# Both output projections as seven block products over float32 quadrants in SBUF, and the next layer's first unit started at its second token half

## The chip, the cores and the metric

One core of a Trainium2 chip runs the whole program. The metric is the time that the device needs for one execution, in microseconds (us); a profile of one execution shows where it goes. TensorE (PE in the profile, with PEld for its weight loads) multiplies, VectorE (DVE), ScalarE (ACT) and GpSimd (POOL) do everything elementwise, and SyncE (SP) and ACT issue the DMAs.

## The reference

A decoder trunk of two layers on 1024 tokens of width 1024, in float32. Each layer normalises its input, multiplies it with a wide input matrix, runs several gated branches (attention, a short convolution in layer 0, cross-attention to 256 memory tokens) and multiplies their concatenated outputs, 1024 x 2048, with an output matrix:

```python
def odd_layer(h, mem, norm_g, w_in, w_out, ...):
    u = rms_norm(h, norm_g)
    proj = u @ w_in
    ...
    y = jnp.concatenate([yc * jax.nn.silu(cz), yx * jax.nn.silu(xz)], axis=-1)
    return h + y @ w_out
```

`even_layer` ends alike. `h + y @ w_out`, once in each layer, is the output projection.

## The kernel before

All matrix products are made at float32 precision out of float32r matmuls: each operand is split into a high part (ACT copies it to float32r, line 130) and a low part (the difference, line 131, on VectorE or GpSimd), and three products, high x high, high x low and low x high, are added up in PSUM. So each 128x128x512 piece of a product costs three matmuls.

The stages follow each other in program order: `run` goes through layer 0's eight heads of differential attention with the convolution groups between them, two pairs of cross-attention heads (`x_pair`), then `out_proj`; then layer 1's twelve heads, its two pairs and its `out_proj`. A scheduler orders the instructions of each engine by priority and readiness; each engine then runs its queue strictly in that order, and so do the DMA queues of SP and ACT. A tile that shares a buffer (same tag) with an older one waits until the older one's readers are done.

`u`, the normalised input, lies transposed in four tiles of 16 KB a partition (tag `u`: high and low parts, two token halves). A unit of an input projection reads it: `token_unit` for queries, keys and values (lines 200 to 202), `feature_unit` for gates and convolution (233 to 235), which goes over a token half at a time.

The attention writes its gated outputs `y` to DRAM (`y_dr`, in tiles of 256 tokens by 512 features). In layer 0 the first eight heads still have to be multiplied with a per-token norm (`on_dr`), which is loaded as a tile `rn` repeated over all partitions.

`out_proj` goes over the output's left half of columns two token blocks at a time, then over the right half a token block at a time. For each token block `out_blocks` loads four tiles of y (`yr`, on ACT's queue), multiplies them with `rn` where needed (GpSimd, line 753), splits them (ACT, VectorE) and issues 48 matmuls (lines 760 to 762). The left half's weights go into the four `u` tiles, and the first four of their sixteen chunks already into small free tiles during the last pair of cross-attention heads (`out_early`, called from `x_pair`). The right half's weights are loaded and split during the first half, into 32 tiles `wo`. The residual is loaded as `hb`, added to the PSUM bank (784, 802) and stored. After each token block of the right half in layer 0, `norm_rows` and `turn_rows` normalise the finished rows and transpose them into the next layer's `u`. The last block's transposes follow the third block of layer 1's first unit.

PSUM has eight banks under four tags: `d` 3, `s` 2, `t` 2, `o` 1. The attention uses `s` for scores, `t` for transposes and `o` for its output `po`, which VectorE gates (`y`, line 453) before the next `po` may start.

Of the kernel before, what the change touches and what calls it, by code (L numbers as in the profile page):

```python
# [7 lines left out]
F32 = mybir.dt.float32  # L8
# [25 lines left out]
class Trunk:  # L34
    def __init__(self, ctx, tc, io):
# [24 lines left out]
        self.queue, self.groups, self.boot, self.turn_last = [], 0, True, None  # L60
# [79 lines left out]

    def turn_rows(self, xn, dst_hi, dst_lo):

        nc = self.nc
        for j in range(2):
            tp = self.bank("pt", "t")
            for i in range(4):
                c = 4 * j + i
                nc.tensor.transpose(tp[:, i * P:(i + 1) * P], xn[:, c * P:(c + 1) * P], self.ident)
# [40 lines left out]
    def token_unit(self, weights, lhs_hi, lhs_lo, nblk, post, together=False):  # L189
# [5 lines left out]
        for t0 in range(0, nblk, step):  # L195
            blks = [(tb, self.bank("pd", "ds"[tb % 2] if together or self.boot else "d"), lhs_hi(tb), lhs_lo(tb)) for tb in range(t0, t0 + step)]
# [9 lines left out]
            if self.turn_last is not None and t0 == 2:  # L206
                with self.tc.issue_after(mm.ins):
                    self.turn_last()
                self.turn_last = None
# [246 lines left out]
    def qkv_unit(self, w, cols, ng, gs, g, extra=None, pairs=False, weights=None):  # L456
# [3 lines left out]
        qns = []  # L460

        def post(tb, ps):
            raw = self.evac(ps, 384 if extra is None else 396)
            qns.append(self.qk_norm(raw, ng, gs))
# [4 lines left out]
            if tb % 2:  # L469
                if pairs:  # L470
                    self.later(DEFER, lambda: self.qk_transpose_pairs(qns[tb - 1:tb + 1], (qh, ql), (kh, kd, kl, kz), g, (tb - 1) * P))
                else:
                    self.later(DEFER, lambda: self.qk_transpose(qns[tb - 1:tb + 1], [(qh, ql, g), (kh, kl, None)], (tb - 1) * P))
        if weights is None:
            weights = self.unit_weights(w, [(c, P) for c in cols] + ([] if extra is None else [extra[0]]), None if extra is None else (nc.vector, nc.gpsimd))
        self.token_unit(weights, self.u_lhs(0), self.u_lhs(1), NB, post)
# [112 lines left out]
    def x_pair(self, layer, pr, w, cq, cz, w_out):  # L589
# [23 lines left out]
        if pr == 1:  # L613
            self.out_early(w_out)
# [100 lines left out]
    def out_weights(self, w, half, tiles, chunks, raws):  # L715

        nc = self.nc
        for c in chunks:
            raw = raws()
            nc.sync.dma_start(out=raw, in_=w[c * P:(c + 1) * P, half * 512:(half + 1) * 512])  # L720
            self.split(tiles(0, c), tiles(1, c), raw, nc.vector if c % 2 else nc.gpsimd)

    def raw_tile(self):
        return self.pa.tile([P, 512], F32, name="wraw", tag="raw", bufs=4)

    def out_early(self, w):

        early = [[], []]
        for part, n in enumerate(("kd", "kz") if self.ptb == 2 else ("kd", "kd")):
            early[part].append(self.att_half(n))  # L730
            early[part].append(self.pk.tile([P, 512], F32R, name="we", tag="gate", bufs=2))
        for t in ("c1", "bias"):
            two = self.pk.tile([P, T + 4] if t == "c1" else [P, T], F32R, name="we", tag=t, bufs=1)
            for part in range(2):
                early[part].append(two[:, part * 512:(part + 1) * 512])
        self.early = early
        self.out_weights(w, 0, lambda part, c: early[part][c], range(len(early[0])), self.raw_tile)

    def out_blocks(self, layer, tbs, tiles, fetch=None):

        nc = self.nc
        pss = [self.bank("pd", "s" if i % 2 and tb > 1 else "d") for i, tb in enumerate(tbs)]
        for j in range(4):
            if fetch is not None:
                fetch(range(4 * j, 4 * j + 4))
            for tb, ps in zip(tbs, pss):
                ts = slice(tb * P, (tb + 1) * P)
                yr = self.pk.tile([P, 4, P], F32, name="yr2", tag="yr", bufs=4)
                nc.scalar.dma_start(out=yr, in_=self.y_dr[layer][tb // 2][j][tb % 2])
                if layer == 0 and j < 2:  # L750
                    rn = self.pa.tile([P, 4, P], F32, name="rn", tag="hs", bufs=3)
                    nc.scalar.dma_start(out=rn, in_=self.on_dr[j][tb].unsqueeze(0).broadcast_to([P, 4, P]))
                    nc.gpsimd.tensor_tensor(out=yr, in0=yr, in1=rn, op=ALU.mult)
                yh = self.pa.tile([P, 4, P], F32R, name="yh2", tag="wfh", bufs=3)
                yl = self.pa.tile([P, 4, P], F32R, name="yl2", tag="wfl", bufs=3)
                self.split(yh, yl, yr, nc.vector)
                for i in range(4):
                    c = 4 * j + i
                    h, l = tiles(0, c), tiles(1, c)
                    nc.tensor.matmul(ps, lhsT=yh[:, i, :], rhs=h, start=(c == 0), stop=False)  # L760
                    nc.tensor.matmul(ps, lhsT=yh[:, i, :], rhs=l, start=False, stop=False)  # L761
                    self.last_mm = nc.tensor.matmul(ps, lhsT=yl[:, i, :], rhs=h, start=False, stop=(c == 15))  # L762
        return pss

    def out_proj(self, layer, w, res, dst, g_next):
        nc, tc = self.nc, self.tc
        with tc.tile_pool(name=f"p2_{layer}", bufs=1, reuse_waits="tile") as p2:

            self.new_u()
            u, early = self.u, self.early  # L770
            ne = len(early[0])
            w0 = lambda part, c: early[part][c] if c < ne else u[part][(c - ne) // 8][:, (c - ne) % 8, :]
            ws = [[p2.tile([P, 512], F32R, name=f"wo{p}_{c}") for p in range(2)] for c in range(16)]
            w1 = lambda part, c: ws[c][part]

            gb = p2.tile([P, D], F32, name="gb2")
            hbs = [p2.tile([P, D], F32, name=f"hb{i}") for i in range(4)]
            for tbs in ((tb, tb + 1) for tb in range(0, NB, 2)):
                fetch = (lambda cs: self.out_weights(w, 0, w0, [c for c in cs if c >= ne], self.raw_tile)) if tbs[0] == 0 else None
                rows = [hbs[tb // 2 % 2][:, tb % 2 * 512:(tb % 2 + 1) * 512] for tb in tbs]  # L780
                for tb, rs in zip(tbs, rows):
                    nc.sync.dma_start(out=rs, in_=res[tb * P:(tb + 1) * P, :512])
                for tb, rs, ps in zip(tbs, rows, self.out_blocks(layer, tbs, w0, fetch)):
                    nc.vector.tensor_tensor(out=rs, in0=ps, in1=rs, op=ALU.add)
                    nc.sync.dma_start(out=dst[tb * P:(tb + 1) * P, :512], in_=rs)
# [110 lines left out]
```

## Time and profile before

| | us |
|---|---|
| median of 3 runs (2209.40 to 2213.86) | 2212.77 |
| the profiled execution | 2208.35 |
| its span, first to last instruction | 2206.6 |
| layer 0's output projection, first to last matmul | 923.3 to 1117.3 |
| layer 1's output projection, first matmul to the last's start | 2020.2 to 2202.4 |

The page gives each engine's busy time, its share of the span and its instructions; the chain of waits follows the work back from the end. A group or a row of the timeline names line, engine, operation, output and inputs, then the shape; `[2.78 <-ACT ex]` behind it is the time the engine stood idle before it and what ended that. Matmuls overlap, so a matmul's price is the distance from start to start, not its duration. The windows view gives busy times by stretch, and the granted TensorE clock as a share of full speed.

### The profile page before, as it was taken

How to read it: one execution, taken by the hardware profiler on the slowest of the kernel's cores; microseconds unless marked ns; L12 is line 12 of the kernel's file. 1: busy time of each engine (PE TensorE's matmuls, PEld its weight loads, DVE VectorE, ACT ScalarE, POOL GpSimd, SP SyncE). 2: the span in 40 equal slices, each digit the busy share in tenths (PEclk: the TensorE clock that was granted, in tenths of full speed). 3: DMA queues.
4: the chain of work that ended last, by engine and by line, in shares of the span. 5: the costliest groups of instructions: out<-in, count | busy, mean ns of one | idle time of the engine just before them, and what ended most of it. 6: DMA issues, size and time to landing. Idle time of an engine off the chain costs nothing.

```text
span 2206.6 us, 35844 instructions
## 1 busy us (share of the span) xinstructions
PE 2170.4 (98%) x12528; PEld 1971.3 (89%) x12528; DVE 1250.3 (57%) x2864; ACT 1057.1 (48%) x2503; POOL 1021.0 (46%) x1352
## 2 busy tenths in 40 slices
PE   7999999999999999999989999999999999999999
PEld 7889889899898899778879999999999999998887
DVE  5646756665665667654535555555555555566432
ACT  6656455464564555432334444444444444455321
POOL 4564655554655453343235555544555554522100
PEclk9999999999999999999999999999999999999999
DMA  5450220211202112486522222211222221223743
GB/s 163 147 146 20 61 57 17 70 50 31 66 24 57 41 54 85 136 274 192 184 49 50 58 58 58 58 35 47 47 56 67 58 58 33 57 76 111 234 132 101
DMA packets 222108, 183.05 MB, mean 83 GB/s; under 512 B 24636, under 2 KB 179420, under 8 KB 221928
## 3 DMA queue, kind: packets, MB, share of 16 engines
q1 hardware_dynamic: 198888, 138.82, 22.1%
q10 hardware_dynamic: 23040, 41.95, 6.1%
q8 instruction: 98, 1.61, 0.3%
q14 instruction: 82, 0.67, 0.1%
HBM read 153.32 MB, written 27.38 MB: 82 GB/s over the span
## 4 chain that ended last, share of the span: by engine, by line
PE 92%; DMA 3%; DVE 2%; POOL 1%; issue 1%; ACT 1%; SPq 0%; ACTq 0%; POOLq 0%; DVEq 0%
PE pd L201 12%; PE pd L202 12%; PE pd L200 12%; PE pss L393 8%; PE pd L234 7%; PE pd L233 7%; PE pd L235 7%; PE pd L762 5%; PE pd L760 5%; PE pd L761 5%; PE pt L427 4%; PE po L441 2%; PE po L442 2%; PE po L440 2%; PE pt L282 1%
## 5 line engine op out<-in xcount | busy, mean ns | idle before, releaser
L200 PE MATMUL pd<-wqh,u 128*128 128x384 f32 (+2 forms) x1536 | 515.1, 336 | 4.0 <-ACT wqh L130 2.8
L201 PE MATMUL pd<-wql,u 128*128 128x384 f32 (+2 forms) x1536 | 514.4, 335 | 2.3 <-DVE wql L131 2.3
L202 PE MATMUL pd<-wqh,u 128*128 128x384 f32 (+2 forms) x1536 | 513.1, 334 | 0.0
L200 PEld LDWEIGHTS pd<-wqh,u 128*128 128x128 f32 x1536 | 291.1, 190 | 8.2 <-ACT wqh L130 3.5
L201 PEld LDWEIGHTS pd<-wql,u 128*128 128x128 f32 x1536 | 291.2, 190 | 7.2 <-DVE wql L131 2.6
L202 PEld LDWEIGHTS pd<-wqh,u 128*128 128x128 f32 x1536 | 291.1, 190 | 4.5
L233 PE MATMUL pd<-u,wfh 128*128 128x512 f32 x704 | 278.1, 396 | 0.0
L234 PE MATMUL pd<-u,wfl 128*128 128x512 f32 x704 | 278.1, 395 | 0.0
L235 PE MATMUL pd<-u,wfh 128*128 128x512 f32 x704 | 277.8, 395 | 0.0
L131 POOL TENSOR_TENSOR wql<-raw,wqh 128x384 fp32r<-128x384 f32 (+2 forms) x216 | 213.9, 1002 | 85.1 <-ACT wqh L130 81.3
L273 DVE TENSOR_TENSOR qr<-qr,rs_r 128x256 f32<-128x256 f32 x200 | 137.8, 689 | 100.9 <-POOL rs_r L124 99.1
L130 ACT ACTIVATE yh<-yr 128x512 fp32r<-128x512 f32 x128 | 80.6, 631 | 219.8 <-PE pd L761 120.4
L130 ACT ACTIVATE pth<-pt 128x512 fp32r<-128x512 f32 (+1 forms) x232 | 122.0, 556 | 131.0 <-PE pt L427 124.2
L124 POOL TENSOR_TENSOR rs_r<-rs_v,neghalf 128x2 f32<-128x2 f32 (+2 forms) x220 | 177.1, 806 | 14.0
L131 DVE TENSOR_TENSOR yl<-yr,yh 128x512 fp32r<-128x512 f32 x128 | 100.1, 782 | 145.9 <-ACT yh L130 127.5
L697 POOL TENSOR_TENSOR fbias<-ck,cqn 128x896 f32<-128x896 f32 (+3 forms) x96 | 110.4, 1150 | 155.8 <-DVE mx L410 123.5
L130 ACT ACTIVATE wqh<-raw 128x384 fp32r<-128x384 f32 (+2 forms) x256 | 118.3, 481 | 118.6 <-DMA raw<-in_e_w_in_dram 59.3
L131 POOL TENSOR_TENSOR wfl<-rawf,wfh 128x512 fp32r<-128x512 f32 x88 | 121.1, 1378 | 107.0 <-ACT wfh L130 106.3
L131 DVE TENSOR_TENSOR ptl<-pt,pth 128x512 fp32r<-128x512 f32 (+1 forms) x232 | 143.7, 639 | 43.8 <-ACT pth L130 41.7
L131 POOL TENSOR_TENSOR vl<-qr,vh 128x128 fp32r<-128x128 f32 x160 | 80.2, 508 | 171.0 <-ACT vh L130 163.9
L235 PEld LDWEIGHTS pd<-u,wfh 128*128 128x128 f32 x704 | 132.3, 188 | 27.3 <-issue 1.1
L234 PEld LDWEIGHTS pd<-u,wfl 128*128 128x128 f32 x704 | 132.5, 188 | 26.3 <-issue 1.4
(277 smaller groups left out, 4974.1 us busy)
## 6 DMA issues: line engine op xcount, KB each, us to landing
yr<-y_dr ACTq DMA_DIRECT2D x128, 256.0 KB
raw<-in_o_w_in_dram SPq DMA_DIRECT2D x288, 64.0 KB
rawf<-in_e_w_in_dram SPq DMA_DIRECT2D x56, 256.0 KB
y_dr<-y SPq DMA_DIRECT2D x112, 128.0 KB
raw<-in_e_w_in_dram SPq DMA_DIRECT2D x192, 64.0 KB
wraw<-in_e_w_out_dram SPq DMA_DIRECT2D x32, 256.0 KB
rn<-on_dr ACTq DMA_DIRECT2D x32, 256.0 KB
rawf<-in_o_w_in_dram SPq DMA_DIRECT2D x32, 256.0 KB
```

The source lines that it names most:

```text
L124: nc.gpsimd.tensor_tensor(out=r[:, :n], in0=v[:, :n], in1=self.neghalf[:, :n], op=ALU.pow)
L130: nc.scalar.activation(out=hi, in_=src, func=AF.Copy)
L131: lo_eng.tensor_tensor(out=lo, in0=src, in1=f32(hi), op=ALU.subtract)
L200: nc.tensor.matmul(ps[:, :n], lhsT=ah(k), rhs=h, start=(k == 0), stop=False)
L201: nc.tensor.matmul(ps[:, :n], lhsT=ah(k), rhs=l, start=False, stop=False)
L202: mm = nc.tensor.matmul(ps[:, :n], lhsT=al(k), rhs=h, start=False, stop=(k == KC - 1))
L233: nc.tensor.matmul(ps, lhsT=h, rhs=uh[:, k, :], start=(k == 0), stop=False)
L234: nc.tensor.matmul(ps, lhsT=l, rhs=uh[:, k, :], start=False, stop=False)
L235: nc.tensor.matmul(ps, lhsT=h, rhs=ul[:, k, :], start=False, stop=(k == KC - 1))
L273: nc.vector.tensor_tensor(out=v, in0=v, in1=r.unsqueeze(2).broadcast_to([P, ng, gs]), op=ALU.mult)
L393: nc.tensor.matmul(ps, lhsT=q[qb // 4][rows, qs], rhs=k[c0 // 512][rows, ks], start=(i == 0), stop=(i == n - 1))
L697: nc.gpsimd.tensor_tensor(out=b[:, :kext], in0=ck[:, :kext], in1=self.cqn[:, qb, h:h + 1].broadcast_to([P, kext]), op=ALU.subtract)
```

## The change

Each projection Y W (1024x2048 by 2048x1024) is cut into quadrants: a11, a12, a21, a22 of Y (512 tokens by 1024 features) and b11, b12, b21, b22 of W (1024 features by 512 columns). Eight quadrant products become seven, by the variant of Strassen's scheme that makes fifteen sums of quadrants:

- product 1: a11 b11; product 2: a12 b21; their sum is the output's quadrant c11
- product 3: S2 T2 with S1 = a11 - a21, S2 = a22 - S1, T1 = b22 - b12, T2 = b11 + T1 (in the code's signs; `a21`, `b12`, `b11` are overwritten)
- product 4: S1 T1; product 5: (a11 + S2)(b22 - T2); product 6: a22 (b21 - T2); product 7: (a12 - a22 + S1) b22

All eight quadrants stay in SBUF as float32, four in the `u` tiles, four in a pool that takes the place of the attention's tiles. Each product goes over eight chunks of 128 features: `a_form` and `b_form` split a chunk of both operands just ahead of its twelve matmuls (four token blocks by three terms), in `product`. The sums of quadrants are made a chunk at a time, by functions `ahead` (the chunk's sums for this or a later product) and `t1`, `t4`, on VectorE and GpSimd. Partial results stand in `q1`, `u2`, `c11`, `c22`, to which the residual is added. `out_early` and its call are gone. The products take all eight PSUM banks, four and four in turn.

```diff
-    def out_weights(self, w, half, tiles, chunks, raws):
...
-    def out_early(self, w):
...
-    def out_blocks(self, layer, tbs, tiles, fetch=None):
...
+            ut = dict(tag="u", bufs=4)
+            a11, b11, b21, a21 = ya(self.up, "a11", **ut), wb(self.up, "b11", **ut), wb(self.up, "b21", **ut), ya(self.up, "a21", **ut)
+            a12, a22, b12, b22 = ya(p2, "a12"), ya(p2, "a22"), wb(p2, "b12", tag="b12", bufs=1), wb(p2, "b22")
+            q1, u2, c11, c22 = (p2.tile([P, 4, 512], F32, name=n) for n in ("q1", "u2", "c11", "c22"))
+            def load_y(t, half, kh):
+                for jj in range(2):
...
+                    if layer == 0 and kh == 0:
+                        for c in range(4 * jj, 4 * jj + 4):
+                            rn = self.pk.tile([P, 4, P], F32, name="rn", tag="gate", bufs=2)
+                            nc.sync.dma_start(out=rn, in_=self.on_dr[jj][4 * half:4 * half + 4, c % 4, :].unsqueeze(0).broadcast_to([P, 4, P]))
+                            nc.gpsimd.tensor_tensor(out=t[:, :, c, :], in0=t[:, :, c, :], in1=rn, op=ALU.mult)
...
+            def a_form(src):
...
+                self.split(h, l, src, nc.vector)
+            def b_form(src):
...
+                self.split(h, l, src, nc.gpsimd)
+            def product(banks, a, b, also=None):
+                for c in range(KC):
+                    if also is not None:
+                        also(c)
+                    (ah, al), (bh, bl) = a_form(a(c)), b_form(b(c))
+                    for tb, ps in enumerate(banks):
+                        nc.tensor.matmul(ps, lhsT=ah[:, tb, :], rhs=bh, start=(c == 0), stop=False)
+                        nc.tensor.matmul(ps, lhsT=ah[:, tb, :], rhs=bl, start=False, stop=False)
+                        nc.tensor.matmul(ps, lhsT=al[:, tb, :], rhs=bh, start=False, stop=(c == KC - 1))
...
+            bx = [self.bank("pd", t) for t in "dddo"]
+            by = [self.bank("pd", t) for t in "sstt"]
+            product(bx, lambda c: a11[:, :, c, :], lambda c: b11[:, c, :])
...
+            for tb in range(4):
+                nc.scalar.activation(out=q1[:, tb, :], in_=bx[tb], func=AF.Copy)
+                tt(nc.gpsimd, c11[:, tb, :], q1[:, tb, :], residual(tb, 0), ADD)
+            def ahead(c):
+                tt(nc.vector, a21[:, :, c, :], a11[:, :, c, :], a21[:, :, c, :], SUB)
+                tt(nc.gpsimd, b12[:, c, :], b22[:, c, :], b12[:, c, :], SUB)
+                tt(nc.vector, b11[:, c, :], b11[:, c, :], b12[:, c, :], ADD)
+            product(by, lambda c: a12[:, :, c, :], lambda c: b21[:, c, :], ahead)
...
+            def ahead(c):
+                s2[c] = tmp([P, 4, P])
+                tt(nc.vector, s2[c], a22[:, :, c, :], a21[:, :, c, :], SUB)
+                tt(nc.gpsimd, a11[:, :, c, :], a11[:, :, c, :], s2[c], ADD)
+            product(bx, lambda c: s2[c], lambda c: b11[:, c, :], ahead)
...
+            def ahead(c):
+                tt(nc.vector, a12[:, :, c, :], a12[:, :, c, :], a22[:, :, c, :], SUB)
+                tt(nc.vector, a12[:, :, c, :], a12[:, :, c, :], a21[:, :, c, :], ADD)
+            product(by, lambda c: a21[:, :, c, :], lambda c: b12[:, c, :], ahead)
+            for tb in range(4):
+                tt(nc.vector, q1[:, tb, :], by[tb], u2[:, tb, :], ADD)
+                tt(nc.gpsimd, c22[:, tb, :], q1[:, tb, :], residual(4 + tb, 1), ADD)
+                tt(nc.gpsimd, q1[:, tb, :], q1[:, tb, :], residual(4 + tb, 0), ADD)
+                tt(nc.gpsimd, u2[:, tb, :], u2[:, tb, :], residual(tb, 1), ADD)
...
+            product(bx, lambda c: a11[:, :, c, :], t1)
...
+            def ahead(c):
+                if c < 6:
+                    b22l.append(self.att_half(("kd", "kz")[c % 2]))
+                    self.split(b22h[:, c, :], b22l[c], b22[:, c, :], nc.vector)
...
+            product(by, lambda c: a22[:, :, c, :], t4, ahead)
```

Product 7 goes a token block at a time, with `b22`'s parts kept for all four. In layer 0 its matmuls are mixed with the norms and transposes of the next layer's input, which begin with token blocks 4 to 7, since their rows are finished by product 6. So layer 1's first unit takes blocks 4 to 7 first (`order` in `token_unit`) and the last transposes follow its blocks (`steps`).

Three places show how the work stands now. The first is VectorE in layer 1 at the end of the attention. `y` is the attention's gated output, `ptl`, `al` and `yl2` are low parts, `u1x` weights.

```order
L453 SCALAR_TENSOR_TENSOR y_24927<-po_24911,xgate_24753 128x256
L131 TENSOR_TENSOR u10_25195<-wraw_25338,u00_25193 128x512
L131 TENSOR_TENSOR yl2_25311<-yr2_25308,yh2_25310 128x512
L131 TENSOR_TENSOR u11_25196<-wraw_25382,u01_25194 128x512
L131 TENSOR_TENSOR yl2_25345<-yr2_25342,yh2_25344 128x512
L131 TENSOR_TENSOR u11_25196<-wraw_25390,u01_25194 128x512
L453 SCALAR_TENSOR_TENSOR y_24970<-po_24954,xgate_24675 128x256
```

That was before; this is the changed kernel:

```order
L464 SCALAR_TENSOR_TENSOR y_24883<-po_24867,xgate_24610 128x256
L131 TENSOR_TENSOR ptl_25003<-pt_24997,pth_25002 128x512
L131 TENSOR_TENSOR ptl_25046<-pt_25040,pth_25045 128x512
L756 TENSOR_TENSOR a21_25109<-a11_25106,a21_25109 128x4x128 x8
L464 SCALAR_TENSOR_TENSOR y_24926<-po_24910,xgate_24688 128x256
L464 SCALAR_TENSOR_TENSOR y_24969<-po_24953,xgate_24610 128x256
L131 TENSOR_TENSOR ptl_25089<-pt_25083,pth_25088 128x512
L464 SCALAR_TENSOR_TENSOR y_25012<-po_24996,xgate_24688 128x256
```

Eight sums that need all of `a21` stand between two of the attention's last outputs, where splits of weights and y tiles stood.

The second is GpSimd in layer 1 around the end of product 1; `bl` from `b21` are product 2's low parts, one for each chunk. Before, GpSimd had these splits of weights in the whole of the projection's first half:

```order
L131 TENSOR_TENSOR u11_25196<-wraw_25386,u01_25194 128x512
L131 TENSOR_TENSOR wo1_0_25198<-wraw_25432,wo0_0_25197 128x512
L131 TENSOR_TENSOR wo1_2_25202<-wraw_25442,wo0_2_25201 128x512
L131 TENSOR_TENSOR wo1_4_25206<-wraw_25600,wo0_4_25205 128x512
L131 TENSOR_TENSOR wo1_6_25210<-wraw_25610,wo0_6_25209 128x512
```

Now, between the second and the fourth chunk of product 2:

```order
L131 TENSOR_TENSOR bl_25365<-b21_25108,bh_25364 128x512
L756 TENSOR_TENSOR b12_25112<-b22_25113,b12_25112 128x512 x2
L756 TENSOR_TENSOR c11_25116<-q1_25114,rs_25319 128x512
L756 TENSOR_TENSOR c11_25116<-q1_25114,rs_25323 128x512
L131 TENSOR_TENSOR bl_25388<-b21_25108,bh_25387 128x512
L756 TENSOR_TENSOR c11_25116<-q1_25114,rs_25327 128x512
L756 TENSOR_TENSOR c11_25116<-q1_25114,rs_25331 128x512
L756 TENSOR_TENSOR a11_25106<-a11_25106,form_25526 128x4x128
L756 TENSOR_TENSOR b12_25112<-b22_25113,b12_25112 128x512 x2
L756 TENSOR_TENSOR a11_25106<-a11_25106,form_25549 128x4x128
L131 TENSOR_TENSOR bl_25411<-b21_25108,bh_25410 128x512
```

The third chunk's low part stands behind four sums, the first of them with `b12` and `b22`, and the fourth chunk's behind seven more.

The third is GpSimd in layer 0 within product 1, where `bl` from `b11` are that product's low parts:

```order
L748 TENSOR_TENSOR a11_11781<-a11_11781,rn_11798 128x4x128
L131 TENSOR_TENSOR bl_11846<-b11_11782,bh_11845 128x512
L131 TENSOR_TENSOR bl_11866<-b11_11782,bh_11865 128x512
L131 TENSOR_TENSOR bl_11886<-b11_11782,bh_11885 128x512
L748 TENSOR_TENSOR a11_11781<-a11_11781,rn_11801 128x4x128
L748 TENSOR_TENSOR a11_11781<-a11_11781,rn_11804 128x4x128
L748 TENSOR_TENSOR a11_11781<-a11_11781,rn_11809 128x4x128
L748 TENSOR_TENSOR a11_11781<-a11_11781,rn_11812 128x4x128
L748 TENSOR_TENSOR a11_11781<-a11_11781,rn_11815 128x4x128
L131 TENSOR_TENSOR bl_11906<-b11_11782,bh_11905 128x512
```

The first multiplication (with rn_11795) stands just ahead of these rows. The fourth chunk's low part comes behind the seventh multiplication with `rn`; all sixteen `rn` tiles pass through two buffers, on SP's queue between the weights.

More of the change, by code (lines that the diff above doesn't have):

```diff
@@ L739, in out_blocks @@
-    def out_blocks(self, layer, tbs, tiles, fetch=None):
[L741 to L763, printed above, removed]
@@ L765, in out_proj @@
     def out_proj(self, layer, w, res, dst, g_next):
         nc, tc = self.nc, self.tc
+        ADD, SUB = ALU.add, ALU.subtract
         with tc.tile_pool(name=f"p2_{layer}", bufs=1, reuse_waits="tile") as p2:
[L769 to L785, printed above, removed]
-                    self.out_weights(w, 1, w1, range(2 * tb, 2 * tb + 2), self.raw_tile)
+            ya = lambda pool, n, **k: pool.tile([P, 4, KC, P], F32, name=n, **k)
@@ new lines, in t4 @@
+            def t4(c):
+                t = tmp([P, 512])
+                tt(nc.vector, t, b21[:, c, :], b11[:, c, :], SUB)
+                return t
+            product(by, lambda c: a22[:, :, c, :], t4, ahead)
+            for tb in range(4):
+                tt(nc.vector, q1[:, tb, :], by[tb], q1[:, tb, :], ADD)
+                store(q1[:, tb, :], 4 + tb, 0)
+            for c in (6, 7):
+                b22l.append(self.pa.tile([P, 512], F32R, name="bl", tag="raw", bufs=4))
+                self.split(b22h[:, c, :], b22l[c], b22[:, c, :], nc.vector)
```

157 lines of the change are left out of this document (104 added, 53 removed).

## The prediction

> **What bounds the kernel now.** I read the page's busy times and its chain first, then the two projection stretches by windows, then single rows at their edges.
>
> ```profile
> PE 2170.4 (98%) x12528; PEld 1971.3 (89%) x12528; DVE 1250.3 (57%) x2864; ACT 1057.1 (48%) x2503; POOL 1021.0 (46%) x1352
> ...
> PE 92%; DMA 3%; DVE 2%; POOL 1%; issue 1%; ACT 1%; SPq 0%; ACTq 0%; POOLq 0%; DVEq 0%
> ```
>
> TensorE is the bound: 98% busy, 92% of the chain. So an edit pays by the matmuls it takes away, unless it makes TensorE wait. The two projections, by windows (length, then busy time of PE, PEld, DVE, ACT, POOL, then granted clock, DMA share, GB/s):
>
> ```profile
> 923.30:1117.40 194.10, 190.71 (x851) 154.03 (x850) 96.81 (x118) 64.39 (x112) 61.86 (x55) 0.99 0.65 207
> 2020.20:2202.80 182.60, 182.60 (x809) 148.77 (x807) 70.14 (x102) 54.45 (x92) 16.65 (x12) 1.00 0.52 166
> ```
>
> Layer 0's stretch has 3.4 us without PE work, layer 1's none; the vector engines are half idle or more. There is nothing to win here but matmuls, and there is room on the other engines to lose. The price of a matmul, from the timeline:
>
> ```profile
> 1099.82 0.39 PE L761 MATMUL pd<-wo,yh 128*128 128x512 f32 x1
> ...
> 1104.97 0.40 PE L762 MATMUL pd<-wo,yl 128*128 128x512 f32 x1
> 1105.21 1.04 PE L148 MATMUL pt<-ident,xn 128*128 128x128 f32 x8
> 1106.00 0.48 PE L760 MATMUL pd<-wo,yh 128*128 128x512 f32 x1
> ```
>
> From the first to the 23rd row 5.15 us pass: 0.234 us each. Eight transposes take 0.79.
>
> **The change part by part.** *Matmuls.* A projection falls from 768 matmuls of 512 columns to 672 (7 products x 8 chunks x 4 blocks x 3 terms): 192 fewer in both layers, **-44.9 us**. A chunk (12 matmuls) is 2.8 us of PE, a product 22.5.
>
> *What feeds a chunk.* Before, a weight was split once and a y tile twice. Now every product makes both operands' high and low parts again, and the sums of quadrants besides. Counted over products 1 to 6 of a layer, VectorE gets 120 tensor operations of 128x512 with both inputs in SBUF (56 low parts of y, 56 sums, 8 low parts of b22) and GpSimd 80 (48 low parts of weights, 16 sums, 16 with the residual), 96 in layer 0 with `rn`. Their prices, minimum/median/maximum ns:
>
> ```profile
> L753 POOL TENSOR_TENSOR yr<-yr,rn x32: 1271/1295/1754, 920.9 to 1094.6; 128x512 f32<-128x512 f32 x32
> L131 DVE TENSOR_TENSOR yl<-yr,yh x128: 677/692/1782, 923.2 to 2194.9; 128x512 fp32r<-128x512 f32 x128
> ```
>
> The maxima are what matters. The timeline shows when they come, VectorE first, GpSimd beneath:
>
> ```profile
> 972.67 3.47 DVE L131 TENSOR_TENSOR wo<-wraw,wo 128x512 fp32r<-128x512 f32 x2
> ...
> 979.56 0.68 DVE L784 TENSOR_TENSOR hb<-pd,hb 128x512 f32<-128x512 f32 x1
> 980.16 1.20 DVE L131 TENSOR_TENSOR yl<-yr,yh 128x512 fp32r<-128x512 f32 x1
> 981.29 3.48 DVE L131 TENSOR_TENSOR wo<-wraw,wo 128x512 fp32r<-128x512 f32 x2
> ```
>
> ```profile
> 973.86 5.12 POOL L753 TENSOR_TENSOR yr<-yr,rn 128x512 f32<-128x512 f32 x3
> ...
> 979.51 1.30 POOL L131 TENSOR_TENSOR wo<-wraw,wo 128x512 fp32r<-128x512 f32 x1 [0.54 <-ACT wo L130]
> ```
>
> Where both have such work they take turns: 1.74 us for one of each (3.47/2, 5.12/3). The operation with PSUM as an input (979.56) runs at 0.68 beside GpSimd, and the next starts 0.60 later. So I price a pair at 1.74, of which VectorE has 0.60 and GpSimd 1.14, and a VectorE operation with a PSUM input does not count. A layer then needs 120 x 0.60 + 80 x 1.14 = 163 us (layer 0: 72 + 109 = 181) of this shared resource within six products that are 135 us on PE. Alone, that is more than the matmuls removed.
>
> The Trainium skill, "SBUF — State Buffer", section "SBUF: two separate sides", says that VectorE and GpSimd arbitrate for one port pair with an exclusive lock for the whole instruction, so that the loser fully blocks. By it a pair would cost 0.69 + 1.29 = 1.98, an estimate that would add some 14% to the shared sums here; the trace's 1.74 is used.
>
> *By product.* Products 1 to 3 have 60 GpSimd operations in layer 0 (16 `rn`, 24 low parts, 4 `c11`, 8 `b12`, 8 `a11`) and 66 on VectorE (24 low parts, 8 each of `a21`, `b11` and S2, 16 on `a12`, 2 of T1): 60 x 1.14 + 66 x 0.60 = 108 us; layer 1, without `rn`, 90. PE needs 67.5. Product 5 has 8 low parts and 12 residual adds on GpSimd and 22 operations on VectorE: 36 against 22.5; with 2 to 4 us of slack in product 6, **+9 a layer** (bounds 5 and 14). Products 4 (14 us) and 6 (20 us) stay under PE. Product 7 has no GpSimd tensor work; its transposes are the old ones in another order: 0.
>
> *Arrival in layer 1.* Early weights are gone: everything is loaded when `u` and the attention's tiles come free.
>
> ```profile
> 2012.71 0.39 PE L235 MATMUL pd<-u,wfh 128*128 128x512 f32 x1
> ...
> 2020.01 0.39 PE L235 MATMUL pd<-u,wfh 128*128 128x512 f32 x1
> 2020.23 0.39 PE L760 MATMUL pd<-kd,yh 128*128 128x512 f32 x1
> ```
>
> ```profile
> 960.00:980.00 20.00, 17.55 (x73) 13.02 (x72) 12.58 (x13) 7.55 (x13) 9.73 (x7) 1.00 0.91 313
> 2060.00:2080.00 20.00, 20.00 (x87) 15.95 (x86) 9.76 (x15) 8.17 (x15) 6.00 (x6) 1.00 0.96 326
> ```
>
> The last gate unit stops reading `u`'s second half at 2013 and its first half at 2020. At 0.32 MB/us (DMA share 0.91 to 0.96), a11, b11, b21 and a21 (8.4 MB) are in at about 2039. On VectorE the eight `a21` sums stand ahead of the last five `y` of the attention (the order above), so GpSimd and PE have only chunks 0 to 2 of three banks until 2041.6; the fourth bank has the tag of the attention's `po`. Each further `po` group follows the `y` before it:
>
> ```profile
> 919.71 0.58 PE L440 MATMUL po<-pth,kd 128*128 128x256 f32 x1 [0.36 <-DVE y L453]
> ...
> 921.88 0.58 PE L440 MATMUL po<-pth,kd 128*128 128x256 f32 x1 [0.52 <-DVE y L453]
> ```
>
> 2.17 us apart: the attention ends near 2050, and only then b22, b12 and a22 can be fetched (their tiles, or their y). PE's remaining 69 matmuls of product 1 end at 2066.6; b12's first part comes at 2050.5 + 4.7 MB / 0.32 = 2065, and GpSimd waits for it ahead of product 2's third chunk. From there 34 GpSimd and 48 VectorE operations stand before product 3's last chunk: 34 x 1.74 + 14 x 0.60 = 67.6, then 2.8: 2135. PE alone would be there at 2020.2 + 67.5 + 4.5 of attention = 2092: **+43**. If all arrivals hid, the shared sum would give 2020 + 90 + 2.8, so +21.
>
> *Arrival in layer 0.* Loads start at 907.7 in the same way.
>
> ```profile
> 907.46 0.40 PE L235 MATMUL pd<-u,wfh 128*128 128x512 f32 x1
> ...
> 918.34 0.58 PE L393 MATMUL pss<-kd,kh 128*128 128x256 f32 x1 [2.78 <-ACT ex L630]
> ...
> 923.33 0.63 PE L760 MATMUL pd<-kd,yh 128*128 128x512 f32 x1
> ```
>
> Two `rn` tiles are at hand; the third stands on SP's queue behind 3.1 MB of weights, half the rate being ACT's queue's, so at about 929, and each later one waits for a multiplication two before it. GpSimd has product 1's fourth low part behind the seventh multiplication: about 948, where PE would be at 932. Behind it are 50 GpSimd operations up to product 3's last low part: 50 x 1.74 = 87, then 2.8: 1038, against 923.3 + 67.5 + 1.5 = 992: **+46**; the shared sum alone, from 917, +36.
>
> *The rest.* The 3.4 us of idle time in layer 0 go with the old order: -3.4. The opening of layer 1's first unit waits for its first weights now:
>
> ```profile
> 1117.33 1.04 PE L148 MATMUL pt<-ident,xn 128*128 128x128 f32 x8
> 1120.56 0.81 PE L200 MATMUL pd<-wqh,u 128*128 128x396 f32 x3 [2.19 <-ACT wqh L130]
> 1123.66 0.70 PE L201 MATMUL pd<-wql,u 128*128 128x396 f32 x1 [2.29 <-DVE wql L131]
> ```
>
> Afterwards the same splits stand behind the norms of the last token blocks on ACT and VectorE, and the order of token blocks gives them product 7 as cover but for the last: I take 0, between -5 and +4. Stores and the last add stay.
>
> *Sum.* The walks count every wait in full, the shared sums none; the order is fixed, so I go nearer to the walks: +42 for layer 0 and +38 for layer 1. 42 + 38 + 9 + 9 - 44.9 - 3.4 = +50. The profiled execution took 2208.35 us, 4.4 below the runs' median (2212.77, all within 4.5); on the execution's own time the forecast is **2258 us**. Less than 0.2% (4.4 us) is no change that a measurement could tell.
>
> **The rivals.** *It is faster, since the new work hides.* It decides at the pair: if VectorE and GpSimd did not hold each other up, GpSimd alone (1.29 each) would set layer 0's first three products at 77 us (+10) and product 5 at 25.8 (+3 a layer), layer 1's would fit under PE but for half of the arrival (+11): 2208 - 48 + 27 = 2187. For it: VectorE is 38 to 50% busy in the windows and the median operation takes 0.69. Against it: every row where both are at it shows 1.74. 12%.
>
> *Half clock on top.* TensorE with many short waits also loses clock:
>
> ```profile
> 925.46 0.63 PE L760 MATMUL pd<-we,yh 128*128 128x512 f32 x1
> 925.89 0.63 PE L761 MATMUL pd<-we,yh 128*128 128x512 f32 x1
> ```
>
> Seven us after the idle 2.78 a matmul still takes 0.43, so a chunk 5.1. If the waits of products 1 to 3 keep it there for half of the 48 chunks and a third of these is exposed, 8 x 2.3 = 18, and as much again where it reaches products 5 and 7: 2295. The Trainium skill, "TensorE: Matmul & The Clock Gate", section "Part 1: The HAM clock gate", halves the clock after an idle window of about 3.4 us and gives it back after a busy one as long; by it the price would end sooner than in these rows, so the rows are used. 15%.
>
> *The waits just eat the gain* (no change): half of the shared sum slips into products 4, 6 and 7. Room there is some 10 us a layer, so it would need the arrivals to cost nothing too: 2208. 5%.
>
> **How the numbers follow.** Forecast 68%, half clock 15%, faster 12%, no change 5%. Slower by over 0.2%: 83%, within 5%, faster 12%. The range goes from 2214 (shared sums with arrivals nearly free, and layer 1's opening better) to 2304 (walks in full with some half clock); it leaves out the faster rival and the far ends.
>
> **What would show it.** PE's matmuls of the projections 1344 instead of 1536, at 0.234 where nothing waits; VectorE's low parts at 1.2 to 1.7 us on average, not 0.69; PE busy well under 90% between the starts of products 1 and 4 in both layers, and idle time put down to GpSimd's `bl` and VectorE's `al`; in layer 1 a gap of some 10 us where PE waits for `y`. I am wrong if VectorE's operations stay at 0.7 beside a busy GpSimd, or if the gaps are there but end within 10 us a layer.

## The result, and the profile after

The changed kernel takes 2292.67 us (median of 4 runs, 2292.26 to 2296.13), the kernel before 2211.88 beside it: ratio 1.0369, 95% interval 1.0351 to 1.0387. The profiled execution took 2292.27, 83.9 us more than that of before.

The page of the changed kernel, busy times and the chain by engine:

```profile
PE 2158.5 (94%) x12336; PEld 1949.3 (85%) x12336; DVE 1425.1 (62%) x2976; ACT 1074.9 (47%) x2559; POOL 1209.4 (53%) x1472
...
PE 82%; DVE 6%; DMA 4%; issue 3%; POOL 3%; ACT 1%; SPq 0%; DVEq 0%; POOLq 0%; ACTq 0%
```

TensorE has 192 matmuls less and is still the bound, but 10% of the chain has gone over to other engines. The windows of the changed kernel show where: layer 0's products 1 to 3, product 4 and product 5, then layer 1's products 1 to 3 and product 5 (columns as before):

```profile
920.90:1055.20 134.30, 86.88 (x326) 65.87 (x327) 100.83 (x87) 33.82 (x61) 95.28 (x61) 0.82 0.47 159
1055.20:1077.00 21.80, 21.80 (x98) 18.03 (x97) 11.43 (x12) 13.29 (x24) 10.41 (x9) 1.00 0.00 0
1077.00:1110.30 33.30, 26.03 (x97) 19.79 (x96) 31.85 (x25) 8.15 (x14) 30.11 (x20) 0.90 0.15 48
2068.00:2184.30 116.30, 86.51 (x328) 66.11 (x329) 88.46 (x84) 32.38 (x58) 71.58 (x45) 0.84 0.44 156
2206.10:2240.80 34.70, 26.33 (x98) 20.47 (x97) 32.89 (x26) 9.04 (x15) 31.52 (x21) 0.85 0.14 46
```

Product 4 is what a product takes when nothing waits: 21.8 us, 0.227 a matmul. Three products are 65.4, and layer 0 needs 134.3, layer 1 116.3. In product 5 VectorE and GpSimd are both over 90% busy and TensorE is not.

The low parts of the changed kernel that are made of a quadrant itself (those made of a sum in a `form` tile have rows of their own), by line (minimum, median, maximum ns), VectorE's and GpSimd's:

```profile
L131 DVE TENSOR_TENSOR al<-a,ah x96: 675/1343/1814, 921.6 to 2278.8; 128x512 fp32r<-128x512 f32 x96
L131 POOL TENSOR_TENSOR bl<-b,bh x64: 1262/1714/1767, 921.5 to 2198.1; 128x512 fp32r<-128x512 f32 x64
```

VectorE's median low part went from 692 ns (`yl` before) to 1343 (`al`). In product 2 of layer 1 the two engines run like this, VectorE first:

```profile
2121.33 3.44 DVE L756 TENSOR_TENSOR a<-a,a 128x512 f32<-128x512 f32 x2
...
2122.51 3.38 POOL L756 TENSOR_TENSOR c<-q,rs 128x512 f32<-128x512 f32 x2
```

One of each in 1.7 us. And at the end of layer 1's attention, TensorE, VectorE, ACT:

```profile
2087.68 0.58 PE L451 MATMUL po<-pth,vh 128*128 128x256 f32 x1 [11.12 <-DVE y L464]
...
2084.80 2.50 DVE L756 TENSOR_TENSOR a<-a,a 128x512 f32<-128x512 f32 x4 [2.86 <-DMA a<-y_dr]
2087.21 0.42 DVE L464 SCALAR_TENSOR_TENSOR y<-po,xgate 128x256 f32<-128x256 f32 x1
...
2089.16 12.11 ACTq L742 DMA_DIRECT2D a<-y_dr  x4
2101.38 0.63 ACT L130 ACTIVATE ah<-a 128x512 fp32r<-128x512 f32 x1 [11.62 <-DMA a<-y_dr]
```

TensorE waits 11.1 us for `y`, which stands behind the `a21` sums, which wait for `a21`. Then ACT stands at the issue of the four loads of `a12`, and the high part of product 1's fourth chunk is behind them.

### The profile page after: what moved, and what is told of

Read it like the earlier page. It is cut to its first block, busy times and chain, and to the rows that moved or that the text cites. A ratio compares the mean times of both kernels' runs of the same rounds, so it can differ in the third digit from the quotient of the medians.

```text
span 2290.5 us, 35537 instructions
## 1 busy us (share of the span) xinstructions
PE 2158.5 (94%) x12336; PEld 1949.3 (85%) x12336; DVE 1425.1 (62%) x2976; ACT 1074.9 (47%) x2559; POOL 1209.4 (53%) x1472
## 4 chain that ended last, share of the span: by engine, by line
PE 82%; DVE 6%; DMA 4%; issue 3%; POOL 3%; ACT 1%; SPq 0%; DVEq 0%; POOLq 0%; ACTq 0%
PE pd L214 11%; PE pd L215 11%; PE pd L213 11%; PE pss L404 7%; PE pd L245 7%; PE pd L244 7%; PE pd L246 7%; PE pt L438 4%; PE po L452 2%; PE po L453 2%; PE po L451 2%; PE pd L781 2%; PE pd L780 2%; PE pd L779 2%; DVE al L131 1%
## 5 line engine op out<-in xcount | busy, mean ns | idle before, releaser
L284 DVE TENSOR_TENSOR qr<-qr,rs_r 128x256 f32<-128x256 f32 x200 | 136.3, 682 | 101.4 <-POOL rs_r L124 99.8
L780 PE MATMUL pd<-bl,ah 128*128 128x512 f32 x384 | 160.1, 424 | 34.3 <-POOL bl L131 34.1
L124 POOL TENSOR_TENSOR rs_r<-rs_v,neghalf 128x2 f32<-128x2 f32 (+2 forms) x220 | 178.2, 810 | 13.9
L779 PE MATMUL pd<-bh,ah 128*128 128x512 f32 x384 | 132.6, 417 | 36.1 <-ACT ah L130 35.1
L781 PE MATMUL pd<-bh,al 128*128 128x512 f32 x384 | 154.1, 422 | 13.1 <-DVE al L131 12.9
```

The costliest lines, as they stand in the source:

```text
L124: nc.gpsimd.tensor_tensor(out=r[:, :n], in0=v[:, :n], in1=self.neghalf[:, :n], op=ALU.pow)
L779: nc.tensor.matmul(ps, lhsT=ah[:, tb, :], rhs=bh, start=(c == 0), stop=False)
L780: nc.tensor.matmul(ps, lhsT=ah[:, tb, :], rhs=bl, start=False, stop=False)
L781: nc.tensor.matmul(ps, lhsT=al[:, tb, :], rhs=bh, start=False, stop=(c == KC - 1))
```

## The experiments

Times of products are distances between the first matmuls of products in the timeline; all in us. TensorE alone needs 21.8 for product 1 and 43.5 for two products. The times of the changed kernel and of 1, 9 and 10 are medians of four runs, which lie 3 to 9 us apart; the others ran once, so a difference of a few us between two of them shows nothing by itself.

| kernel | time | layer 0: p1 | p2+3 | p5+6 | layer 1: p1 | p2+3 | p5+6 |
|---|---|---|---|---|---|---|---|
| changed | 2292.67 | 51.3 | 83.0 | 57.4 | 47.8 | 68.5 | 58.2 |
| 1 all on VectorE | 2246.40 | 49.4 | 64.7 | 51.7 | 48.7 | 53.9 | 51.7 |
| 2 a21 after attention | 2288.87 | 50.4 | 83.0 | 57.4 | 46.0 | 69.0 | 58.2 |
| 3 without rn | 2279.47 | 51.2 | 69.4 | 57.8 | 51.0 | 68.5 | 58.2 |
| 4 a12, a22 on SP | 2284.07 | 43.8 | 82.8 | 59.8 | 46.3 | 68.7 | 58.2 |
| 5 unread GpSimd work | 2297.78 | 52.9 | 77.8 | 59.8 | 48.9 | 68.5 | 60.0 |
| 6 loads behind stores | 2273.28 | 38.6 | 82.2 | 59.8 | 33.9 | 74.7 | 58.2 |
| 7 paced sums | 2215.37 | 50.6 | 55.2 | 46.7 | 47.2 | 43.5 | 46.2 |
| 8 all together | 2208.47 | 36.3 | 64.5 | 48.6 | 30.5 | 51.4 | 46.7 |
| 9 rn in free tiles | 2195.63 | 38.7 | 54.8 | 46.7 | 32.2 | 51.7 | 46.7 |
| 10 b21 earlier | 2198.71 | 40.3 | 50.1 | 48.3 | 37.6 | 45.2 | 48.3 |
| 11 GpSimd beside | 2269.56 | 49.8 | 56.8 | 46.8 | 47.6 | 88.7 | 45.8 |

**1. All on VectorE.**

```diff
-                self.split(h, l, src, nc.gpsimd)
+                self.split(h, l, src, nc.vector)
-                tt(nc.gpsimd, b12[:, c, :], b22[:, c, :], b12[:, c, :], SUB)
+                tt(nc.vector, b12[:, c, :], b22[:, c, :], b12[:, c, :], SUB)
...
```

> All low parts and sums of the seven products go to VectorE; GpSimd keeps only the multiplications with rn in layer 0. Taking turns (theory: a VectorE and a GpSimd operation with SBUF inputs cost 1.74 us together, VectorE alone 0.60): 200 operations x 0.60 = 120 us for products 1 to 6 against 131 us of matmuls, so products 2 and 3 fall from 83.0 us (layer 0) and 68.5 us (layer 1) to about 56 and 46, product 5 from 33.3 and 34.7 to about 25; product 1 stays, since its loads set it. In all about -65 us: 2225 to 2235, VectorE's low parts at 0.7 us. Rival (the two engines do not hold each other up, the sheer number of operations is too much): VectorE with 200 x 0.69 = 138 us is a tighter bound than before, 2293 to 2310.

Measured 2246.40 (4 runs, ratio to before 1.0162, interval 1.0136 to 1.0188): 46 us won by giving one engine more work and the other nearly none of these products. VectorE's low parts by line (median 686 ns again), and the window of layer 1's products 2 and 3:

```profile
L131 DVE TENSOR_TENSOR al<-a,ah x96: 677/686/1759, 921.0 to 2231.7; 128x512 fp32r<-128x512 f32 x96
```

```profile
2089.70:2143.60 53.90, 47.34 (x193) 36.68 (x193) 53.43 (x89) 20.87 (x35) 0.00 (x0) 0.94 0.15 54
```

VectorE is busy in 53.4 of 53.9 us: it is now the bound there. The 2225 to 2235 expected had left out its operations with a PSUM input, 24 a layer, and what the order costs (experiment 7). This run takes away the shared access and GpSimd's own time together (77 us for layer 0's first three products at the 1.29 of the prediction), so it doesn't say how the 46 us divide between them.

**2. The a21 sums behind the attention's last y.**

```diff
-        self.nc.vector.scalar_tensor_tensor(out=y, ...)
+        self.last_y = self.nc.vector.scalar_tensor_tensor(out=y, ...)
...
-                tt(nc.vector, a21[:, :, c, :], a11[:, :, c, :], a21[:, :, c, :], SUB)
+                with self.tc.issue_after(self.last_y.ins):
+                    tt(nc.vector, a21[:, :, c, :], a11[:, :, c, :], a21[:, :, c, :], SUB)
```

> The eight a21 sums are issued on VectorE behind the attention's last y. Theory (they hold up the attention's y while they wait for a21): the 11.1 us that TensorE waits for y in layer 1 goes, the attention ends near 2086 and product 1's fourth chunk starts near 2092 instead of 2102; layer 0 as it was: about -10 us, 2283. Rival (the loads of a12, b12, a22 end last anyway): the fourth chunk comes earlier, but product 2 waits longer; 2290 to 2293.

Measured 2288.87; product 1 of layer 1 gained 1.8 us, not 10. VectorE and SP's queue in this kernel's timeline, then two of its windows:

```profile
2083.15 0.42 DVE L464 SCALAR_TENSOR_TENSOR y<-po,xgate 128x256 f32<-128x256 f32 x1 [7.95 <-DMA y_dr<-y]
...
2075.13 11.00 SPq L460 DMA_DIRECT2D y_dr<-y  x4
```

```profile
2070.00:2075.00 5.00, 4.40 (x28) 3.69 (x26) 1.61 (x3) 1.19 (x2) 0.00 (x0) 1.00 1.05 386
2075.00:2080.00 5.00, 0.00 (x0) 0.00 (x0) 0.20 (x1) 0.00 (x0) 0.00 (x0) 0.91 1.05 387
```

The same `y` is late, but for another reason: it has two buffers, and they are not free until an older `y` has been stored, while the DMA engines are full with 8.4 MB of quadrants (share 1.05). The sums had only stood in front of this wait. ACT's halt is still there too: four issues of 12.3 us, up to 2097.4, hold the fourth chunk 5 us beyond the attention's end.

**3. Without rn.**

```diff
-                    if layer == 0 and kh == 0:
...
-                            nc.sync.dma_start(out=rn, in_=self.on_dr[jj][...].broadcast_to([P, 4, P]))
-                            nc.gpsimd.tensor_tensor(out=t[:, :, c, :], in0=t[:, :, c, :], in1=rn, op=ALU.mult)
```

> Layer 0's sixteen rn tiles are neither loaded nor multiplied (this leaves out the per-token norm of the first eight heads). Theory (the rn chain through two buffers sets product 1 of layer 0, and its sixteen multiplications take 1.14 us each of the shared sum behind it): product 1 from 51.3 to about 32 us, products 2 and 3 from 83.0 to about 69 as in layer 1: -30 to -35 us, 2258 to 2263. Rival (it is the a12 loads on ACT's queue that hold the fourth chunk, rn costs its turns only): -18, 2275.

This kernel leaves out the per-token norm of the first eight heads. Measured 2279.47, nearer the rival. Layer 0's product 1 did not move (51.2), products 2 and 3 fell by 13.6. So rn is not what ends last in product 1, while its multiplications and loads cost 13.6 behind it.

**4. a12 and a22 on SP's queue.**

```diff
-                        nc.scalar.dma_start(out=t[...], ...)
+                        (nc.sync if kh else nc.scalar).dma_start(out=t[...], ...)
```

> a12 and a22 are loaded by SP's queue instead of ACT's. Theory (ACT stands 11 to 12 us at the issues of a12, and the high part of the fourth chunk of product 1 behind them): that chunk starts about 5 us earlier in layer 0 (then GpSimd's seventh multiplication with rn sets it) and 3.5 us earlier in layer 1: 2284 to 2287. Rival (weights, rn and residuals now stand behind a12 on SP's queue): no gain or up to +8, 2292 to 2300.

Measured 2284.07: product 1 is 7.5 us shorter in layer 0, 1.5 in layer 1. What is left in layer 1 is the wait for `y`. ACT's halt was on the path, 9 us in all where 8.5 were forecast, but divided otherwise (5 and 3.5). In layer 0 the fourth chunk now waits for what the prediction had put last, GpSimd's low part behind the seventh multiplication with rn:

```profile
950.53 1.97 PE L780 MATMUL pd<-bl,ah 128*128 128x512 f32 x4 [1.91 <-POOL bl L131]
```

**5. Unread GpSimd work beside experiment 1.**

```diff
                 self.split(h, l, src, nc.vector)
+                nc.gpsimd.tensor_tensor(out=dummy[:, :512], in0=src, in1=f32(h), op=SUB)
```

> As all-on-VectorE, and GpSimd again makes the low part of every weight chunk of products 1 to 6 (48 a layer), into a tile that nobody reads. Theory (taking turns): 48 x 1.14 = 55 us of the shared time come back in each layer, so VectorE's operations go back to 1.7 us beside GpSimd and 30 to 50 us of the gain are lost: 2275 to 2295. Rival (the gain came from the shorter chain of engines, GpSimd does not slow VectorE): 2242 to 2250, VectorE's low parts at 0.7.

Measured 2297.78: all 51 us are back. But it didn't come about as expected. GpSimd and ACT in this kernel's timeline, then VectorE's low parts by line:

```profile
2134.11 22.22 POOL L773 TENSOR_TENSOR dummy<-b,bh 128x512 f32<-128x512 f32 x1 [7.15 <-issue]
...
2156.36 0.63 ACT L130 ACTIVATE bh<-b 128x512 fp32r<-128x512 f32 x1 [9.74 <-POOL dummy L773]
```

```profile
L131 DVE TENSOR_TENSOR al<-a,ah x96: 671/679/1789, 924.2 to 2284.4; 128x512 fp32r<-128x512 f32 x96
```

The median low part stayed at 679 ns. Here it was GpSimd that was held off, for 22 us in one operation, and since it still had to read `bh`, ACT could not reuse that tile. This kernel couples the engines in two ways, so it doesn't settle the price of sharing; experiment 11 does.

**6. Loads behind the attention's stores** (on the changed kernel, with experiment 2's edit; a12, a21 and a22 also go to SP's queue, which takes in experiment 4's).

```diff
-                        nc.scalar.dma_start(out=t[...], ...)
+                        (nc.scalar if t is a11 else nc.sync).dma_start(out=t[...], ...)
...
-            load_y(a12, 0, 1)
-            load_w(b21, 1, 0)
+            with self.tc.issue_after(self.last_store.ins):
+                load_y(a12, 0, 1)
+                load_w(b21, 1, 0)
...
+            with self.tc.issue_after(self.last_store.ins):
+                load_y(a21, 1, 0)
+                load_w(b22, 1, 1)
...
```

> The changed kernel with its GpSimd work, but the a21 sums behind the attention's last y on VectorE, and the loads of a12, b21, a21, b22, b12, a22 on SP behind the attention's last y store; only a11 and b11 (4.2 MB) go ahead of the stores. Theory (what holds up product 1 is that the attention's y, two buffers, cannot be stored while 8.4 MB of quadrants are on the way): product 1 falls from 51.3 and 47.8 to 34 to 38 us, products 2 and 3 stay: 2265 to 2272. Rival (the later loads make products 2 and 3 wait instead): product 1 falls as much, products 2 and 3 grow by the same: 2285 to 2295.

Measured 2273.28, product 1 at 38.6 and 33.9, about as expected. The windows of both layers' product 1:

```profile
921.40:960.00 38.60, 31.87 (x135) 25.61 (x136) 18.22 (x23) 14.31 (x28) 24.09 (x18) 0.87 0.82 267
...
2056.60:2090.50 33.90, 31.06 (x136) 25.40 (x137) 17.49 (x22) 13.95 (x25) 12.53 (x10) 0.90 0.76 264
```

In layer 1 TensorE's longest wait for `y` is now 0.9 us, while in experiment 2, with the sums out of the way too, it was still 9.2: there the burst of quadrants ahead of the attention's stores held up product 1. In layer 0, 7.5 of the 12.7 us are what experiment 4 gained by itself, ACT's halt. Layer 1 gives 6.2 us back in products 2 and 3, whose loads now come later.

**7. Paced sums** (on experiment 1).

```diff
+                        if paced:
+                            with self.tc.issue_after(self.last_al.ins):
+                                also(c)
...
-                tt(nc.vector, q1[:, tb, :], q1[:, tb, :], residual(4 + tb, 0), ADD)
-                tt(nc.vector, u2[:, tb, :], u2[:, tb, :], residual(tb, 1), ADD)
...
```

The two adds come back behind product 6, `c11`'s behind product 4.

> As all-on-VectorE, with the sums for products 3, 4 and 6 issued a chunk at a time between the low parts, and the residual adds of three quadrants behind products 4 and 6. Theory (what is left in all-on-VectorE outside product 1 is bunched sums ahead of low parts that TensorE waits for): products 2 and 3 from 64.8 and 53.9 to about 50 and 46 us, product 5 from 29.9 to about 23: -30 to -36, 2210 to 2216. Rival (VectorE is simply full: 208 operations x 0.60 = 125 us for products 2 to 6 against 109 on TensorE): -10 at most, 2236 to 2246.

Measured 2215.37. Layer 1's products 2 and 3 take 43.5 us, just what the matmuls need, with VectorE almost full:

```profile
2075.90:2119.40 43.50, 43.50 (x194) 36.02 (x193) 42.11 (x70) 19.79 (x35) 0.00 (x0) 1.00 0.09 34
```

The order had cost 31 us over both layers: sums for later products and residual adds stood in bunches ahead of low parts.

**8. All together** (6 and 7, and `a21`'s multiplications with rn on VectorE).

> All on VectorE with paced sums, and the loads behind the attention's stores; layer 0's eight multiplications of a21 with rn on VectorE too. If the causes add up: 2210 less 13 a layer of product 1 = 2185, faster than the kernel before by about 1%. If arrivals and VectorE's load only hide each other: 2205 to 2215, no faster.

Measured 2208.47, the less hopeful case. SP's queue and VectorE of this kernel, at the end of layer 0's product 2:

```profile
971.91 21.62 SPq L747 DMA_DIRECT2D rn<-on_dr  x6
...
991.70 1.45 DVE L748 TENSOR_TENSOR a<-a,rn 128x512 f32<-128x512 f32 x2 [1.50 <-DMA rn<-on_dr]
```

Two buffers for eight rn tiles: each pair is fetched when the pair before it has been multiplied, and VectorE has sums to do in between.

**9 and 10. rn in free tiles; then b21 earlier.**

```diff
-                            rn = self.pk.tile([P, 4, P], F32, name="rn", tag="gate", bufs=2)
+                            rn = ((u2, c22)[jj][:, c % 4, :].rearrange("p (a b) -> p a b", a=4) if half else
+                                  self.pk.tile([P, 4, P], F32, name="rn", tag="gate", bufs=2))
```

> As all-together, but the eight rn tiles for a21 land in the tiles of u2 and c22, which are not used yet, instead of passing two buffers. Theory (in all-together TensorE stands about 18 us at the end of product 2 of layer 0, because each pair of rn tiles is fetched only when the pair before it has been multiplied, behind twelve sums on VectorE): products 2 and 3 of layer 0 from 64.5 to about 52 us, as in layer 1 (51.4): 2196, with layer 1 as it was. Rival (all loads together arrive that late): no change, 2206 to 2209.

> As rn-in-free-tiles, and b21 is loaded behind the fifth last of the attention's stores instead of the last. Theory (from 2030 to 2050 the DMA engines are half idle in all-together and busy to 2080, so everything lands 5 us earlier): products 2 and 3 about 4 us shorter in each layer, product 1 the same: 2188. Rival (the last stores wait behind b21's 2.1 MB again): product 1 4 to 6 us longer in each layer, nothing won, 2196 to 2206.

Measured 2195.63 for the first (4 runs, 2193.51 to 2198.71): ratio to before 0.9932, interval 0.9917 to 0.9947. This version of the change is faster than the kernel before. With `b21` loaded earlier, 2198.71 (0.9931 to 0.9964): products 2 and 3 gain 4.7 and 6.5, product 1 loses 1.6 and 5.4, products 5 and 6 some 1.6. The rival's exchange, at no gain.

**11. GpSimd beside VectorE, on tiles of its own** (on experiment 7).

```diff
+            if layer == 1:
...
+                tt(nc.gpsimd, idle[0], q1[:, 0, :], q1[:, 0, :], SUB)
+                for i in range(63):
+                    tt(nc.gpsimd, idle[1 + i % 5], idle[0], idle[0], ADD)
```

> As paced-sums, and in layer 1 GpSimd makes 64 additions of 128x512 one after the other from the end of product 1 on, on three tiles of its own that no other engine reads or writes. Nothing but the shared SBUF access can couple the engines here, other than in unread-gpsimd, where the copies held the weight tiles. Theory (turns: 0.60 + 1.14 us a pair as long as both have work): the 64 last 111 us, products 2 to 6 of layer 1, which had 111.5 us and no slack on VectorE, take up to 73 us longer: about 2285, VectorE's low parts at 1.7 there. Rival (VectorE's unbroken stream keeps GpSimd off, as in the row of all-on-VectorE where two GpSimd operations took 11.24 us): GpSimd's additions stretch, VectorE stays at 0.7: below 2235.

Measured 2269.56, 54 us over experiment 7, for work that nobody waits for. The first of the 64 operations reads `q1`, the 63 behind it only tiles of their own. The 63 additions by tile, then the timeline of VectorE during them and just after:

```profile
L756 POOL TENSOR_TENSOR idle<-idle x63: 1033/1482/1487, 2079.8 to 2168.4; 128x512 f32<-128x512 f32 x63
```

```profile
2091.76 5.86 DVE L756 TENSOR_TENSOR b<-b,b 128x512 f32<-128x512 f32 x4
...
2168.95 1.52 DVE L756 TENSOR_TENSOR a<-a,a 128x512 f32<-128x512 f32 x1
2170.40 0.68 DVE L131 TENSOR_TENSOR al<-a,ah 128x512 fp32r<-128x512 f32 x1
2171.01 0.68 DVE L756 TENSOR_TENSOR a<-a,a 128x512 f32<-128x512 f32 x1
```

1.45 us from start to start on VectorE while GpSimd works, 0.60 from the moment it stops: 63 x 0.85 = 54. The pair is cheaper than 1.74; this addition, which reads one tile twice, is also shorter by itself (1.03 at its fastest, against 1.26 for a low part).

## Why the prediction was right, and where its sizes were off

The direction, the cause and the range held: 2292.3 against 2258, within 2214 to 2304. The 34 us missing lie in three places: layer 0's projection takes 238.4 us, 19.1 more than forecast (and starts 2.4 earlier), layer 1's 218.6, 11.5 more, and from the one to the other 908.7 us pass instead of 902.8, 5.9 more.

- *Matmuls.* 1344, as said. The price was 0.227 in products 1 to 6 and 0.232 in product 7, not 0.234. In the kernel before, the median distance from start to start is 0.227 in the left halves and 0.234 in the right halves of both layers, and the 5.15 us were read off a right half. So without waits both projections together shrink by some 48 us instead of 44.9, an estimate: 768 x 0.227 + 768 x 0.234 before, 1152 x 0.227 + 192 x 0.232 after. Why the halves differ is open.
- *The shared access.* "A pair at 1.74": 1.7 in the trace, and experiment 11 isolates it. It is the largest item that the runs single out, as moving GpSimd's part to VectorE is worth 46 us, though that takes GpSimd's own time away too. It doesn't decide the change alone: with it gone the kernel is still 1.6% slower than before, until the order (31 us) and the loads are mended. The count of 120 operations for VectorE holds 8 low parts of product 7; products 1 to 6 have 112, and the sums by product go by the right counts. The claim of the Trainium skill, "SBUF — State Buffer", section "SBUF: two separate sides", that the one who loses waits for the whole instruction of the other, agrees in kind with the rows where the two alternate; the pitch of 1.7 is below the 1.98 that was worked out with it, and the last section has a wait of many instructions.
- *Layer 1, products 1 to 3.* The walk (+43) gives 114.8 us, the windows show 116.3; 5 of it were given away by booking +38. The wait for `y` was said to be some 10 us and is 11.1. But of its cause the prediction had half: experiment 2 takes the `a21` sums out of the way and the wait stays, for the stores; experiment 6 shows that both hang on the same burst of loads. That the walk comes so near is in part luck: it has product 1 last 46.4 us (47.8 measured) by the attention alone, while in the trace the attention is through at 2096.5 and ACT's halt, which the walk lacks, holds the fourth chunk until 2101.4.
- *Layer 0, products 1 to 3.* Forecast 110.7 (68.7 + 42), measured 134.3: the term that fell. Its step "GpSimd has product 1's fourth low part behind the seventh multiplication" is right as an order and in time (948 forecast, 949.1 measured), but not what ends last. The fourth chunk waits for ACT, which stands at `a12`'s loads until 955.3:

```profile
943.84 11.44 ACTq L742 DMA_DIRECT2D a<-y_dr  x4
949.14 1.26 POOL L131 TENSOR_TENSOR bl<-b,bh 128x512 fp32r<-128x512 f32 x1
955.38 0.63 ACT L130 ACTIVATE ah<-a 128x512 fp32r<-128x512 f32 x1 [13.07 <-DMA rn<-on_dr]
...
1013.93 1.71 POOL L748 TENSOR_TENSOR a<-a,rn 128x512 f32<-128x512 f32 x1
1023.89 1.49 POOL L748 TENSOR_TENSOR a<-a,rn 128x512 f32<-128x512 f32 x1 [8.25 <-DMA rn<-on_dr]
```

  The releaser that ACT's row names, rn, is put down by inference; experiment 3 has no rn and the same 51 us, experiment 4 moves `a12` and gains 7.5. "Behind it are 50 GpSimd operations, 87 us" assumed that GpSimd never waits again: the last two rows (its own in product 2) show an 8 us wait for rn, whose two buffers `form` shares. Experiment 3 puts 13.6 us on rn there. The walk allowed 24.7 us up to the fourth chunk and 90 behind it; the trace has 34.4 and 99.8, and 4 of the walk's +46 had been booked away.
- *Product 5.* +9 a layer, bounds 5 and 14. Products 5 and 6 took 57.4 and 58.2 against 43.5: +13.9 and +14.7, the second just beyond the bound. The slack of 2 to 4 us in product 6 wasn't there; product 6 itself is 2 us longer than its matmuls. On VectorE alone and with most residual adds elsewhere (experiment 7), 3 us remain for both.
- *The opening.* Taken as 0, between -5 and +4. The 5.9 us between the projections are more than that, and 4.8 of them are lost by the first matmul with a low part of a weight, which comes 11.4 us after the projection's last matmul instead of 6.6. Of the two waits for weights the second grew from 2.29 to 4.73:

```profile
1164.93 0.81 PE L213 MATMUL pd<-wqh,u 128*128 128x396 f32 x3 [2.34 <-ACT wqh L130]
1170.48 0.70 PE L214 MATMUL pd<-wql,u 128*128 128x396 f32 x1 [4.73 <-DVE wql L131]
```

  The cover that was counted on is too short: the norms of the last token blocks stand ahead of the weight splits. This is read from the trace; no experiment changed it.
- *The rivals.* "Faster" fell with the pair, "no change" with the waits of products 1 to 3 and 5, which didn't hide. "Half clock on top" gives 2295, next to the result, and its sign is there (clock 0.82 and 0.84 in products 1 to 3). But each experiment that took waits away took half clock with them, so its own share stays open.

## What to carry to other kernels

A scheme that trades matmuls for elementwise work has to be priced on the engines that do that work, with their shared access: here GpSimd beside VectorE was worth less than nothing, and one engine alone did it in less time. Before a stage that fetches everything at once, see what small transfers of the stage before stand in the same queues; and read a wait's row as the last of several, since the next one shows only when it is taken away. With these three mended (one engine, sums in order, loads behind the stores) the same scheme came out level (experiment 8, 2208.47 against 2210.07, one run each). It took rn's free tiles as well to beat the old product, by 0.7%, where the matmuls alone promised 2%.

## What was not expected of the hardware

VectorE and GpSimd don't always take turns. Where GpSimd had one operation after the other waiting, they alternated (1.45 and 1.7 us a pair). Where an operation came to GpSimd singly while VectorE ran without a gap, it waited for a gap: in experiment 1 two multiplications took 11.24 us, in experiment 5 one operation 22.22.

```profile
972.59 11.24 POOL L748 TENSOR_TENSOR a<-a,rn 128x512 f32<-128x512 f32 x2 [14.45 <-DMA rn<-on_dr]
```

What decides between the two isn't settled by these runs. And four DMA issues on ACT's queue held ACT's own work for 11 to 12 us, in both layers.
